# A hybrid decoder layer on one core: another order for the first 125 microseconds

## The chip, the cores and the metric

One core of a Trainium2 chip runs the whole layer. The core has a matmul engine (TensorE, PE in the profile, with PEld for its weight loads), three engines for elementwise work (VectorE or DVE, ScalarE or ACT, GpSimd or POOL) and SyncE (SP), which here issues nearly all the transfers. Each engine works through its own instruction queue in order and waits on semaphores for the others. The metric is the device time of one execution in microseconds.

## The reference

```python
mod = silu(c) @ w_ada + b_ada                 # c: 2048, w_ada: 2048 x 6144
shift, scale, gate = split(mod, 3)
h = rms_norm(x, norm_gain) * (1 + scale) + shift        # x: 1024 tokens x 2048
proj = h @ w_in                                # w_in: 2048 x 8192
# columns: q, k, v, z of 8 stick-breaking heads, then q, k, v, z of 8 retention heads
qa, ka = rms_norm(q_sb) * sb_q_gain, rms_norm(k_sb) * sb_k_gain
oa = stick_breaking_attention(qa, ka, v_sb) * silu(z_sb)
ob = head_group_norm(retention(rotary(q_r), rotary(k_r), v_r)) * silu(z_r)
out = x + gate * (concat(oa, ob) @ w_out)      # w_out: 2048 x 2048
```

Everything is float32. Nothing of h can be had before shift and scale, which need 2048 rows of w_ada, and before the norm of x; and no projection starts before some of h is there.

## The kernel before, in words

**The projections.** A projection is done by a Strassen-Winograd scheme: one `Group` makes 256 output columns for all 1024 tokens over half of the contraction (1024 of 2048), as seven products P1 to P7 of combinations of blocks. The left operands are the seven combinations A11, S2, S3, A12, S1, A22, S4 of h, the right ones combinations of the weights (`RIGHT`, `LEFT`). Each combination of h is cut into four pieces `j` (`NP` = 4) and each piece into a high and a low part in fp32r (`split`: the high part by ScalarE, the low part, the rest, by VectorE), and so are the weights (`first` makes the high part, `second` the low part, `make` the sums). A product of one piece is three matmuls (`mm3`: high by high, high by low, low by high), a product of a group twelve. Products share PSUM banks: P1, P6, P5 and P3 add into bank b, P7 and P4 into d, P2 has bank a; after P1, P6 and P7 ScalarE copies the bank out (`ended`, `copied`) before the next product goes into it. `plan` writes the products of all groups in one list: P1, then P4 and P3 of the group before, then P6, P7, P2, P5. Weights are split two products ahead of their use, with three buffers.

**The opening** is what stands before that list. A piece j of h needs four 512-token by 128-channel tiles xT (two channel blocks, two token halves g), and scale and shift for those 256 channels. The steps:

- 32 tiles of x are loaded (`xt`), each 128 tokens by 512 channels, into places that are later used for the parts of h.
- `x_norms(g)` takes the mean squares of 4 times 128 tokens, half by ScalarE (`Square` with a sum), half by VectorE (`bn_stats`), makes the inverse root by Newton steps on VectorE (`rsqrt_newton`), and puts it on a diagonal (`dg`), in two pairs of 128 tokens.
- `turn_x(kc, g)` transposes four 128 by 128 blocks of x on TensorE against those diagonals, which also multiplies by the norm; ScalarE or, each fourth time, VectorE copies the result to xT.
- For each j, `ada_loads` loads 16 tiles of w_ada ("rows" below: 128 of the 2048 rows of w_ada, 256 columns of shift and 256 of scale). Each is weighed by silu(c): six by VectorE (`ADA_DVE`, `weigh`, line 443) into an accumulator, two by ScalarE with a sum on GpSimd (`ADA_ACT`), eight by TensorE, which sums over its partitions at once (`ada_rows_pe`, line 526). `ada_finish` adds TensorE's one row of sums to the accumulator and sums over partitions by matmuls against ones (`over_partitions`), so that the sums stand in columns; `ada_mod` makes scale and shift from them.
- `first_half(j)` applies them (`to_h`, line 435, on ScalarE), makes the combinations (`combine`, on GpSimd for j up to 2, on VectorE for the last) and the high and low parts (`place`).

The tiles of w_ada share places: eight for block 0, ten for each later block, for sixteen rows. SyncE issues the loads in its queue's order and waits at one whose place isn't free.

**What sets the order.** In the opening only TensorE's instructions run in the order in which they are written; those of the other engines are put in order by a scheduler with its own estimate of the times. From the first `until` on all engines run as written. The list's own work hangs on a count: `tick` is called after each piece of a product, and starts tasks that wait for their turn, among them the second half of w_ada's rows and of h (`second_half`). `prepare(0)` runs those events of the list that lie before its first product: loads of the first two groups' weights, sums and splits.

Of the kernel before, what the change touches and what calls it, by code (L numbers as in the profile page):

```python
# [11 lines left out]
F32 = mybir.dt.float32  # L12
# [28 lines left out]
ADA_DVE = (0, 3, 6, 8, 11, 14)  # L41
ADA_ACT = (5, 13)
# [17 lines left out]
def layer_kernel(ctx, tc, x, c, w_ada, b_ada, norm_gain, w_in, sb_q_gain, sb_k_gain, ret_norm_gain, w_out,  # L60
# [4 lines left out]
    ctx.enter_context(tc.manual_schedule(engines={mybir.EngineType.PE}))  # L65
# [34 lines left out]
    k1 = k1p.__enter__()  # L100
    stp = tc.tile_pool(name="st", bufs=1)
# [5 lines left out]
    silu_c = cons.tile([P, 16], F32, name="silu_c")  # L107
    nc.scalar.activation(silu_c, c_sb, AF.Sigmoid)
    nc.vector.tensor_tensor(silu_c, silu_c, c_sb, op=ALU.mult)

# [9 lines left out]
    nc.scalar.dma_start(rows[66:74, 0:P], ret_norm_gain.rearrange("o (k p) -> (o k) p", p=P))  # L120
    rows_ps = ps.tile([P, P], F32, tag="C", name="rows_ps")
# [82 lines left out]
    def combine(a11, a12, a21, a22, new, sub):  # L204

        s1, s2, s4 = (new(n) for n in ("S1", "S2", "S4"))
        sub.tensor_tensor(s1, a21, a22, op=ALU.add)
        sub.tensor_tensor(s2, s1, a11, op=ALU.subtract)
        sub.tensor_tensor(a21, a11, a21, op=ALU.subtract)
        sub.tensor_tensor(s4, a12, s2, op=ALU.subtract)  # L210
        return {"A11": a11, "S3": a21, "S2": s2, "A12": a12, "S1": s1, "S4": s4, "A22": a22}

# [21 lines left out]
    class Group:  # L234


        def __init__(self, w, k0, col0, name, **more):
            self.w, self.k0, self.col0, self.name = w, k0, col0, name
            self.seed, self.gate, self.put, self.done, self.pool, self.turns = None, (None, None), None, None, None, False
            self.before = None  # L240
            self.__dict__.update(more)
            self.t, self.parts, self.at, self.old, self.tell, self.early = {}, {}, {}, {}, None, None
# [24 lines left out]

    sums = []
# [36 lines left out]
    def plan(groups, lasts):  # L305
# [16 lines left out]
        for k, (g, p) in enumerate(flat):  # L322
            if p == "P1":
                on(k - 7, 0, lambda g=g: g.load(0))
                on(k - 6, 1, lambda g=g: g.load(1))
                sum_of(g, "T3", k - 3, 1)
                alone = g.at["P6"] == k + 1
                sum_of(g, "T2", k - 2 if alone else k - 1, 3 if alone else 1)
# [95 lines left out]
    def ada_mod(j, mod):  # L424
# [6 lines left out]
    ENGINES = [mybir.EngineType.PE, mybir.EngineType.Activation, mybir.EngineType.DVE, mybir.EngineType.Pool,  # L431
               mybir.EngineType.SP]

# [22 lines left out]

    turns = 0

    def turn_x(kc, g):

        nonlocal turns
        tag, bufs = (("pj0", 1), ("A1", 1), ("pj1", 1), ("pj2", 1), ("B", 1), ("pj3", 1))[turns % 6]
        turns += 1
        tp = ps.tile([P, HALF], F32, tag=tag, bufs=bufs, name=f"xtp_{kc}_{g}")
# [14 lines left out]
    def x_norms(g):  # L479
        for t2 in (4 * g, 4 * g + 2):  # L480
            ss = st.tile([P, 4], F32, tag="ss", bufs=2, name=f"ss_{t2}")
            st6 = st.tile([P, 4, 6], F32, tag="st6", bufs=2, name=f"st6_{t2}")
            mv = st.tile([P, 2], F32, tag="mv", bufs=2, name=f"mv_{t2}")
            for qt in range(4):
                junk = st.tile([P, HALF], F32, tag="ht", bufs=7, name=f"junk_{t2}_{qt}")
                nc.scalar.activation(junk, xt[t2, qt], AF.Square, accum_out=ss[:, qt:qt + 1])
            for qt in range(4):
                nc.vector.bn_stats(st6[:, qt, :], xt[t2 + 1, qt])
            nc.vector.bn_aggr(mv, st6)
            m = st.tile([P, 2], F32, tag="m", bufs=2, name=f"m_{t2}")  # L490
            y = st.tile([P, 2], F32, tag="y", bufs=2, name=f"y_{t2}")
            u = st.tile([P, 2], F32, tag="u", bufs=2, name=f"u_{t2}")
            nc.vector.tensor_reduce(m[:, 0:1], ss, axis=mybir.AxisListType.X, op=ALU.add)
            nc.vector.tensor_scalar(m[:, 0:1], m[:, 0:1], 1.0 / D, EPS, op0=ALU.mult, op1=ALU.add)
            nc.vector.scalar_tensor_tensor(m[:, 1:2], mv[:, 0:1], mv[:, 0:1], mv[:, 1:2], op0=ALU.mult, op1=ALU.add)
            nc.vector.tensor_scalar(m[:, 1:2], m[:, 1:2], EPS, None, op0=ALU.add)
            rsqrt_newton(y, m, u)
            for i in range(2):
                dg[t2 + i] = st.tile([P, P], F32, tag="dg", bufs=8, name=f"dg_{t2 + i}")
                nc.vector.tensor_scalar(dg[t2 + i], ident, y[:, i:i + 1], None, op0=ALU.mult)  # L500

    accs, acc2s, for_pe, row_sums = {}, {}, {}, {}

    def ada_loads(j):

        accs[j] = acc = st.tile([P, HALF], F32, tag="acc", bufs=2, name=f"acc_a{j}")
        tags = free[0][:8] if j == 0 else free[j]
        for r in range(16):
            src = hp.tile([P, HALF], F32, tag=tags[r % len(tags)], name=f"ada_a{j}_{r}")
            nc.sync.dma_start(src.rearrange("p (a n) -> p a n", a=2), ada_rows[:, r, 0:2, 256 * j:256 * j + 256])  # L510
            if r in ADA_DVE:
# [855 lines left out]
```

## Time and profile before

| | |
|---|---|
| median of 3 runs | 2012.84 us (2012.56 to 2014.52) |
| the profiled execution | 2010.2 us, of which the profile's span is 2008.4 us |
| granted TensorE clock, mean over the span | 0.983 |
| TensorE busy | 1932.5 us, 96% |
| VectorE busy | 1460.3 us, 73% |
| ScalarE busy | 866.7 us, 43% |
| GpSimd busy | 189.6 us, 9% |
| HBM read and written | 278.51 and 108.10 MB |

The page gives for each engine its busy time, cuts the span into 40 slices of 50 us with busy tenths and the granted clock in tenths, and lists the costliest groups of instructions. A row of the view in order of time has the start, the duration, the engine, the line, the operation, the tile written and those read, the shape, the count of instructions that were merged, and in brackets the idle time of the engine before it and what ended it. Instructions of TensorE overlap, so the distance of their starts is what one costs, not the duration. The table by stretches gives busy times in windows.

### The profile page before, as it was taken

To read this page: it belongs to the slowest core of one execution; us is meant where nothing else is said; L and a number is where in the kernel's file an instruction comes from. 1 tells how busy PE (TensorE), PEld (TensorE's weight loads), DVE (VectorE), ACT (ScalarE), POOL (GpSimd) and SP (SyncE) were. 2 spreads that over 40 slices of the span, in tenths; PEclk is the share of its full clock that TensorE was granted. 3 is DMA by queue.
4 is the path that set the end of the run, shared out by engine and by line. 5 is a ranking of instruction groups with operands and counts; after the bars stand their busy time and mean duration, and the time that the engine had idled before them with its cause. 6 is when DMAs were issued, how large, how long until landed. Compare 5 with 4: busy or idle time off the path is not lost. (4 is left out here: it accounts for less than half of the span.)

```text
span 2008.4 us, 26769 instructions
## 1 busy us (share of the span) xinstructions
PE 1932.5 (96%) x9057; PEld 1557.8 (78%) x9057; DVE 1460.3 (73%) x2598; ACT 866.7 (43%) x1574; POOL 189.6 (9%) x131
## 2 busy tenths in 40 slices
PE   5879999999999999999999999899999998999998
PEld 4368888876778787788888888588888887888887
DVE  6778898685668586766656766688787887568765
ACT  4443333553354544454444444434343445345221
POOL 0311111220000001001000100113021211010000
PEclk9879999999999999999999999899999999999999
DMA  9738988434545455443433534758677887357665
GB/s 298 248 119 274 291 283 300 132 110 125 184 152 156 129 169 185 144 133 108 155 114 124 169 104 131 269 189 287 205 265 242 274 273 259 127 168 262 204 206 167
DMA packets 287325, 388.41 MB, mean 193 GB/s; under 512 B 32106, under 2 KB 164276, under 8 KB 287188
## 3 DMA queue, kind: packets, MB, share of 16 engines
q1 hardware_dynamic: 286784, 386.65, 59.5%
q8 instruction: 72, 1.18, 0.3%
q14 instruction: 65, 0.53, 0.1%
q10 hardware_dynamic: 404, 0.05, 0.0%
HBM read 278.51 MB, written 108.10 MB: 192 GB/s over the span
## 5 line engine op out<-in xcount | busy, mean ns | idle before, releaser
L259 ACT ACTIVATE wh_e_P<-wr_e 128x512 fp32r<-128x512 f32 x560 | 353.0, 631 | 464.5 <-PE b_o L151 55.3
L264 DVE TENSOR_TENSOR wl_e_P<-wr_e,wh_e_P 128x512 fp32r<-128x512 f32 x560 | 402.1, 718 | 90.6 <-ACT wh_e_P L259 89.2
L254 DVE TENSOR_TENSOR wr_e<-wr_e,wr_e 128x512 f32<-128x512 f32 x240 | 167.8, 726 | 1.3
L917 DVE TENSOR_TENSOR_SCAN om<-om 128x128 f32<-128x128 f32 (+2 forms) x96 | 95.8, 998 | 55.7 <-ACT om L908 54.1
L443 DVE SCALAR_TENSOR_TENSOR acc_b<-ada_b,silu_c,acc_b 128x512 f32<-128x512 f32 x120 | 90.0, 750 | 17.9 <-DMA ada_b<-in_w_ada_dram 17.1
L730 POOL TENSOR_TENSOR ld<-ld,ld 128x512 f32<-128x512 f32 x7 | 10.3, 1468 | 980.7 <-DMA ld<-mix_A 980.7
L292 DVE TENSOR_TENSOR pt<-b_f,pt 128x512 f32<-128x512 f32 x64 | 44.1, 689 | 57.4 <-PE b_f L152 57.2
L150 PE MATMUL b_e<-S_h,wh_e_P 128*128 128x512 f32 x192 | 76.5, 398 | 5.7 <-ACT pt L286 5.7
L150 PE MATMUL b_h<-S_h,wh_e_P 128*128 128x512 f32 x192 | 78.1, 407 | 1.5 <-ACT S_h L146 1.5
L152 PE MATMUL b_e<-S_h,wl_e_P 128*128 128x512 f32 x192 | 75.9, 396 | 1.2 <-DVE wl_e_P L264 1.2
L964 PE MATMUL oT<-a,v 128*128 128x256 f32 x320 | 76.8, 379 | 0.0
L150 PE MATMUL b_f<-S_h,wh_e_P 128*128 128x512 f32 x192 | 76.6, 399 | 0.0
L151 PE MATMUL b_h<-S_l,wh_e_P 128*128 128x512 f32 x192 | 76.2, 397 | 0.2 <-DVE S_l L147 0.2
L152 PE MATMUL b_h<-S_h,wl_e_P 128*128 128x512 f32 x192 | 75.9, 395 | 0.3 <-DVE wl_e_P L264 0.3
L151 PE MATMUL b_e<-S_l,wh_e_P 128*128 128x512 f32 x192 | 75.8, 395 | 0.0
L150 PE MATMUL b_g<-S_h,wh_e_P 128*128 128x512 f32 x192 | 75.6, 394 | 0.0
L908 ACT ACTIVATE om<-zp,rq 128x128 f32<-128x128 f32 (+2 forms) x96 | 56.0, 583 | 44.9 <-PE zp L903 39.7
L151 PE MATMUL b_f<-S_l,wh_e_P 128*128 128x512 f32 x192 | 75.0, 390 | 0.0
L152 PE MATMUL b_g<-S_h,wl_e_P 128*128 128x512 f32 x192 | 75.0, 390 | 0.0
L152 PE MATMUL b_f<-S_h,wl_e_P 128*128 128x512 f32 x192 | 75.0, 390 | 0.0
L151 PE MATMUL b_g<-S_l,wh_e_P 128*128 128x512 f32 x192 | 74.9, 390 | 0.0
L286 ACT ACTIVATE pt<-b_e 128x512 f32<-128x512 f32 x48 | 28.8, 599 | 97.2 <-PE b_e L152 94.1
(389 smaller groups left out, 5250.0 us busy)
## 6 DMA issues: line engine op xcount, KB each, us to landing
wr_e<-in_w_in_dram SPq DMA_DIRECT2D x128, 512.0 KB
ada_b<-in_w_ada_dram SPq DMA_DIRECT2D x128, 256.0 KB
part<-pt SPq DMA_DIRECT2D x128, 256.0 KB
pt<-part SPq DMA_DIRECT2D x128, 256.0 KB
fin<-pt SPq DMA_DIRECT2D x128, 256.0 KB
ada_a<-in_w_ada_dram SPq DMA_DIRECT2D x64, 256.0 KB
wr_e<-in_w_out_dram SPq DMA_DIRECT2D x32, 512.0 KB
ld<-fin SPq DMA_DIRECT2D x54, 256.0 KB
```

The source lines that it names most:

```text
L150: nc.tensor.matmul(o, a_hi, b_hi, start=first, stop=False, skip_group_check=True)
L151: nc.tensor.matmul(o, a_hi, b_lo, start=False, stop=False, skip_group_check=True)
L152: nc.tensor.matmul(o, a_lo, b_hi, start=False, stop=last, skip_group_check=True)
L254: eng.tensor_tensor(t[o], t[a], t[b], op=op)
L259: nc.scalar.activation(hi, self.t[RIGHT[p]], AF.Copy)
L264: nc.vector.tensor_tensor(lo, self.t[RIGHT[p]], self.parts[p].bitcast(F32), op=ALU.subtract)
L286: nc.scalar.activation(t, src, AF.Copy, scale=1.0 if gt is None else gt)
L292: nc.vector.tensor_tensor(t, src, t, op=ALU.add)
L443: nc.vector.scalar_tensor_tensor(acc, src, cj, acc, op0=ALU.mult, op1=ALU.add)
L908: nc.scalar.activation(om[:, :n], zp[:, :n], AF.Sigmoid, scale=rq[:, h, 1, i:i + 1])
L917: nc.vector.tensor_tensor_scan(rev, rev, rev, init, op0=ALU.mult, op1=ALU.bypass)
L964: nc.tensor.matmul(ob, v[:, j, :], a[:, cl], start=diag and ib == 0 and b == 0 and j2 == 0, stop=ch == 0 and ib == 2, skip_group_check=True)
```

## The change

It writes the opening anew. All engines run in written order from the start (`manual_schedule` with all five). The steps go into a list `todo` with a time each (`do(us, fn, ...)`), and are written in the order of these times, which count a tile of x or w_ada each 0.8 us (`landed`).

- w_ada: VectorE weighs four rows of a block (1, 4, 7, 10; in block 0 three: 9, 11, 13), TensorE the other twelve (thirteen), ScalarE and GpSimd none. `ada_close` adds VectorE's accumulator to the sums by one more matmul against ones, and ScalarE copies the row of sums; `ada_turn` turns it into columns with four small matmuls instead of `over_partitions`. There is one accumulator place instead of two.
- Norms: one Newton chain for four times 128 tokens instead of two, the squares are written to a PSUM bank, four diagonals instead of eight.
- `first_left` takes the place of `first_half` and `combine`: the combinations are all VectorE's, written between the parts; in the last block VectorE also makes two of the four tiles of h.
- The first group's products come in the order P1, P2, P7, P6, P5, and P1, P2 and P7 run by pieces: pieces 0 and 1, then 2, then 3, between the rows of w_ada. The weights of the first group are loaded between those of blocks 1 and 2, those of the second after block 3; `prepare(1)` splits the weights for the first three products.
- The small constants are loaded ahead of the sigmoid of c on ScalarE's queue. The result tiles (`sums`) have their place from the start.

```diff
-ADA_DVE = (0, 3, 6, 8, 11, 14)
-ADA_ACT = (5, 13)
+ADA_DVE = (1, 4, 7, 10)
+ADA_DVE_0 = (9, 11, 13)
...
-    ctx.enter_context(tc.manual_schedule(engines={mybir.EngineType.PE}))
+    ctx.enter_context(tc.manual_schedule(engines=set(ENGINES)))
...
             flat.append((g, "P1"))
-            if i:
-                flat.extend((groups[i - 1], p) for p in ("P4", "P3"))
+            if not i:
+                flat.extend((g, p) for p in ("P2", "P7", "P6", "P5"))
+                continue
+            flat.extend((groups[i - 1], p) for p in ("P4", "P3"))
             flat.extend((g, p) for p in ("P6", "P7", "P2", "P5"))
...
+    def do(us, fn, *a):
+        todo.append((us, len(todo), lambda: fn(*a)))
+
+    def landed(n):
+
+        return 3.5 + 0.8 * (n + 1)
...
+    def ada_row(j, r):
+
+        src, on_dve = row_tiles.pop((j, r)), ADA_DVE if j else ADA_DVE_0
+        if r in on_dve:
+            if r == on_dve[0]:
+                accs[j] = st.tile([P, HALF], F32, tag="acc", bufs=1, name=f"acc_a{j}")
+            weigh(accs[j], src, r, r == on_dve[0])
+            return
+        if r == 0:
+            row_sums[j] = ps.tile([P, HALF], F32, tag=("C", "A0")[j % 2], name=f"ada_sums{j}")
+        nc.tensor.matmul(row_sums[j][0:1, :], silu_c[:, r:r + 1], src, start=r == 0, stop=False, skip_group_check=True)
+
+    def ada_close(j):
+
+        nc.tensor.matmul(row_sums[j][0:1, :], ones, accs[j], start=False, stop=True, skip_group_check=True)
+        nc.scalar.activation(accs[j][0:1, :], row_sums.pop(j)[0:1, :], AF.Copy)
+
+    def ada_turn(j):
+
+        mod, acc = ps.tile([P, 4], F32, tag="B", name=f"mod_m{j}"), accs.pop(j)
+        for i in range(4):
+            nc.tensor.matmul(mod[:, i:i + 1], acc[0:1, i * P:(i + 1) * P], ones[0:1, :], start=True, stop=True)
+        ada_mod(j, mod)
...
+    def first_left(j, us):
+
+        a11, a21, a12, a22 = (xT[2 * j + e, g] for e in range(2) for g in range(2))
+        last = j == NP - 1
...
+        do(us, to_h, a11, 2 * j)
+        do(us, to_h_dve if last else to_h, a12, 2 * j + 1)
+        do(us + 0.1, place, "A11", j, a11)
+        do(us + 0.2, to_h, a21, 2 * j)
+        do(us + 0.2, to_h_dve if last else to_h, a22, 2 * j + 1)
+        do(us + 0.3, place, "A12", j, a12)
+        do(us + 1.0, lambda: tt(s1, a21, a22, op=ALU.add))
+        do(us + 1.0, lambda: tt(a21, a11, a21, op=ALU.subtract))
+        do(us + 1.1, lambda: tt(s2, s1, a11, op=ALU.subtract))
+        do(us + 1.2, place, "S3", j, a21)
+        do(us + 1.3, place, "S2", j, s2)
+        do(us + 2.0, place, "S1", j, s1)
+        do(us + 3.0, lambda: tt(s4, a12, s2, op=ALU.subtract))
+        do(us + 4.0, place, "A22", j, a22)
+        do(us + 5.0, place, "S4", j, s4)
...
+    x_norms(0, landed(15) + 1)
+    x_norms(1, landed(31) + 1)
     for kc in range(KC):
-        turn_x(kc, 0)
...
+        do(21.5 + 0.56 * kc, turn_x, kc, 0)
+        do(35.0 + 0.5 * kc if kc < KC // 2 else 42.0 + kc - KC // 2, turn_x, kc, 1)
+
+    at_row = [32, 48, 68, 84]
+    for j in range(NP):
+        for r in range(16):
+            us = landed(at_row[j] + r)
+            do(us - 4, ada_load, j, r)
+            do(us + 0.3, ada_row, j, r)
+        us = landed(at_row[j] + 15) + 0.5
+        do(us, ada_close, j)
+        do(us + 1.5, ada_turn, j)
+        do(us + 2.5, lambda j=j, us=us: first_left(j, us + 2.6))
+    for i in range(2):
+        do(landed(63) - 3.9, groups_a[0].load, i)
+        do(landed(99) - 3.9, groups_a[1].load, i)
+    do(landed(63) + 12, prepare, 1)
...
+    do(landed(63) + 14, first_products, (0, 1))
+    do(landed(83) + 11, first_products, (2,))
...
+    first_products((3,))
+    run_to[0] = 3
```

`first_products(js)` runs `mm3` for the pieces js of P1, then of P2, then of P7; with the last piece it also ends each product as `run` does.

More of the change, by code (lines that the diff above doesn't have):

```diff
@@ L100, in layer_kernel @@
     k1 = k1p.__enter__()
+    pp = ctx.enter_context(tc.tile_pool(name="pp", bufs=1))
+    sums = [pp.tile([P, HALF], F32, tag=f"pt{i}", bufs=1, name=f"pt{i}") for i in range(7)]
     stp = tc.tile_pool(name="st", bufs=1)
@@ L202, in layer_kernel @@
     left = {}
[L204 to L211, printed above, removed]
     def place(n, j, src, eng=nc.vector):
@@ new lines, in layer_kernel, with first_products @@
+    do(landed(63) + 12, prepare, 1)
+    def first_products(js):
+        g = groups_a[0]
+        for k, (p, into, i) in enumerate((("P1", "b", 0), ("P2", "a", 3), ("P7", "d", 2))):
+            if js[0] == 0:
+                setattr(g, into, bank(i, f"{into}_{g.name}"))
+            hi, lo = g.parts[p]
+            for j in js:
+                mm3(getattr(g, into), hi[:, j, :], lo[:, j, :], *left[LEFT[p], j], j == 0, j == NP - 1)
+            if js[-1] == NP - 1:
+                ended(g, p)
+                for j in range(NP):
+                    for fn in events.pop((k, j), ()):
+                        fn()
+                tick()
```

150 lines of the change are left out of this document (56 added, 94 removed).

## The prediction

> **What bounds the kernel now.** First the page: engines and clock.
>
> ```profile
> span 2008.4 us, 26769 instructions
> PE 1932.5 (96%) x9057; PEld 1557.8 (78%) x9057; DVE 1460.3 (73%) x2598; ACT 866.7 (43%) x1574; POOL 189.6 (9%) x131
> PEclk9879999999999999999999999899999999999999
> ```
>
> TensorE is the bound over the whole span, but slices 2 and 3 (50 to 150 us) have a clock of 0.8 and 0.7. So I looked at the opening in stretches of 10 us, and in stretches of 2 us where the clock changes (columns: length, busy time of PE, PEld, DVE, ACT, POOL, granted clock, DMA share, GB/s).
>
> ```profile
> 80.00:90.00 10.00, 7.38 (x24) 2.04 (x24) 8.51 (x12) 6.03 (x10) 5.37 (x4) 0.97 0.76 247
> 90.00:100.00 10.00, 5.37 (x18) 3.57 (x18) 9.84 (x13) 3.99 (x7) 2.30 (x2) 0.50 0.46 152
> 100.00:110.00 10.00, 7.59 (x25) 6.22 (x25) 6.40 (x11) 6.94 (x11) 6.32 (x4) 0.50 0.00 1
> 130.00:140.00 10.00, 10.00 (x46) 8.29 (x45) 7.75 (x13) 3.50 (x6) 0.00 (x0) 1.00 0.62 190
> ...
> 88.00:90.00 2.00, 0.53 (x2) 0.00 (x0) 2.00 (x3) 0.96 (x3) 2.00 (x2) 0.87 1.07 374
> 90.00:92.00 2.00, 0.00 (x0) 0.00 (x0) 2.00 (x3) 1.57 (x3) 1.19 (x2) 0.50 0.31 104
> 126.00:128.00 2.00, 2.00 (x8) 1.60 (x7) 0.00 (x0) 0.46 (x1) 0.00 (x0) 0.74 0.16 55
> ```
>
> Between 80 and 110 us VectorE is the fullest engine (9.84 of 10 us), TensorE has holes, and its clock is halved from about 89.5 to 127 us. From 130 us on TensorE is full and does the same work in both kernels. I therefore reduce the question to one mark: the first matmul of the second group's P1, when the first group's P1, P6, P7, P2 and P5 are done whatever their order. TensorE in order of time shows the mark and what comes before it.
>
> ```profile
> 103.91 0.77 PE L150 MATMUL b_e<-A_h,wh_e_P 128*128 128x512 f32 x1
> 107.46 0.63 PE L152 MATMUL b_e<-A_h,wl_e_P 128*128 128x512 f32 x1
> 122.29 0.79 PE L150 MATMUL b_e<-S_h,wh_e_P 128*128 128x512 f32 x1 [5.67 <-ACT pt L286]
> 122.88 0.63 PE L151 MATMUL b_e<-S_l,wh_e_P 128*128 128x512 f32 x1
> 123.31 0.63 PE L152 MATMUL b_e<-S_h,wl_e_P 128*128 128x512 f32 x1
> 127.34 0.40 PE L150 MATMUL d_e<-S_h,wh_e_P 128*128 128x512 f32 x1
> 130.07 0.39 PE L150 MATMUL a_e<-A_h,wh_e_P 128*128 128x512 f32 x1
> 135.51 0.39 PE L150 MATMUL b_e<-A_h,wh_e_P 128*128 128x512 f32 x1
> ```
>
> The mark is at 135.5 us. P6 starts at 122.3; its matmuls start 0.43 us apart (122.88 to 123.31) at half clock, and a product of 12 matmuls takes 2.73 us at full clock (127.34 to 130.07), 0.2275 each.
>
> **Prices of the parts.** TensorE's opening work, in order of time, and SyncE's last load of a w_ada row:
>
> ```profile
> 21.53 22.73 PE L467 MATMUL xtp<-dg,x 128*128 128x128 f32 x188 [5.99 <-DMA x<-in_x_dram]
> 53.99 7.41 PE L467 MATMUL xtp<-dg,x 128*128 128x128 f32 x64
> 61.24 1.84 PE L421 MATMUL mod_m<-ones,acc_a 128*128 128x1 f32 x16
> 63.02 12.18 PE L526 MATMUL ada_sums<-ada_a,silu_c 128*1 128x512 f32 x28
> 78.22 1.02 PE L526 MATMUL ada_sums<-ada_a,silu_c 128*1 128x512 f32 x2 [1.80 <-DMA ada_a<-in_w_ada_dram]
> 87.51 1.02 PE L526 MATMUL ada_sums<-ada_a,silu_c 128*1 128x512 f32 x2 [1.15 <-DMA ada_a<-in_w_ada_dram]
> 93.87 1.86 PE L526 MATMUL ada_sums<-ada_a,silu_c 128*1 128x512 f32 x2 [5.34 <-DMA ada_a<-in_w_ada_dram]
> ...
> 90.99 0.37 SPq L510 DMA_DIRECT2D ada_a<-in_w_ada_dram  x1
> ```
>
> One row of w_ada on TensorE is two matmul instructions: 12.18 / 14 = 0.87 us. One turn of x (turn_x) is eight: (61.24 - 53.99) / 8 = 0.91. ada_turn has four matmuls, eight instructions, where 16 took 1.84: 0.92. A reloaded row can be used 93.87 - 90.99 = 2.9 us after its issue. VectorE and ScalarE, in order of time:
>
> ```profile
> 21.19 0.48 DVE L500 TENSOR_SCALAR dg<-ident,y 128x128 f32<-128x128 f32 x2
> 63.40 0.48 DVE L441 TENSOR_SCALAR acc_a<-ada_a,silu_c 128x512 f32<-128x512 f32 x1
> 63.91 2.33 DVE L443 SCALAR_TENSOR_TENSOR acc_a<-ada_a,silu_c,acc_a 128x512 f32<-128x512 f32 x3
> 118.86 0.68 DVE L147 TENSOR_TENSOR S_l<-S,S_h 128x512 fp32r<-128x512 f32 x1
> 119.47 0.68 DVE L147 TENSOR_TENSOR A_l<-xT,A_h 128x512 fp32r<-128x512 f32 x1
> ...
> 63.52 2.93 ACT L435 ACTIVATE xT<-xT,s_c,a_c 128x512 f32<-128x512 f32 x4 [2.37 <-DVE a_c L428]
> 66.35 1.13 ACT L146 ACTIVATE A_h<-xT 128x512 fp32r<-128x512 f32 x2
> 120.19 0.63 ACT L146 ACTIVATE S_h<-S 128x512 fp32r<-128x512 f32 x1 [2.41 <-DVE A_l L147]
> 121.64 0.60 ACT L286 ACTIVATE pt<-b_e 128x512 f32<-128x512 f32 x1 [0.82 <-DVE S_l L147]
> ```
>
> VectorE: 0.6 an operation (119.47 - 118.86), 0.78 a weighed row, 0.5 a block's first. ScalarE: 0.73 to make h, 0.56 a high part.
>
> **The change part by part, on TensorE's queue.** Rows on TensorE go from 8 a block to 13 in block 0 and 12 after: 49 in all instead of 32. That alone is 17 x 0.87 = 14.8 us more on the engine that in the new order also has to do everything else in sequence. What it saves is on engines with room: two rows of ScalarE and their sum on GpSimd, two or three rows of VectorE.
>
> (1) Start. The four factors of tokens 0 to 511 now come from one Newton chain after the sixteenth tile of x, as the later pair's do now (21.19, 0.24 each); two more of them make it 21.8 for a start that is now at 21.53.
>
> (2) To the end of ada_close(1): 32 turns x 0.91 = 29.1; 13 + 12 rows x 0.87 = 21.8; two closes at a row's price, 1.7; ada_turn(0), 0.9. The first matmuls run at half speed, by the tile's own windows:
>
> ```profile
> 22.00:24.00 2.00, 2.00 (x11) 2.00 (x11) 0.00 (x0) 0.60 (x1) 1.00 1.05 385
> 25.00:27.00 2.00, 2.00 (x20) 2.00 (x19) 0.23 (x1) 0.39 (x2) 1.00 1.05 393
> ```
>
> (11 against 20 in 2 us, though the clock column says 1.00): some 1.4 us for the first three. Sum 54.9, so 76.7. The close needs VectorE's row 10, which is written behind the 11 operations that place block 0, an evacuation and two rows: an estimate of 0.8 us late, 77.5.
>
> (3) ada_turn(1) waits for ScalarE's copy (0.6 and hand-over, 0.7), then 0.92: 79.1.
>
> (4) Then the queues bite. TensorE goes on with seven rows of block 2 and stands at row 11 at 79.1 + 7 x 0.87 = 85.2. Row 11 uses the buffer of row 1, which is VectorE's, and VectorE's row 1 is written behind block 1's A11 and A12 and its three sums and S3, S2. That is: bias and scale 0.45, ScalarE's four to_h and two high parts 4.0, VectorE's A12 low part and three sums 2.4, two low parts with a short wait 1.35, the row 0.5: done at 87.8. SyncE waits there with that load; rows 12 to 15, block 3's rows and group 1's weights queue behind it. Plus 2.9: row 11 is there at about 90.8, and TensorE has idled 5.6 us.
>
> (5) After that the clock is halved, as after 88.53 us now. From 122.29 it took 4.4 us to recover, so I charge 2.2. Rows 11 and 12, 18 product matmuls for blocks 0 and 1 (4.1), rows 13 to 15, the close, block 3's row 0 and ada_turn(2) are 11.1: 90.8 + 11.1 + 2.2 = 104.1. VectorE's five operations for the first three weights (prepare) end at about the same time as row 11 comes; if their cover went, they would cost up to 3.4.
>
> (6) Eight rows, block 2's nine matmuls (2.05), three rows, the close: 12.5. Two waits of the kind in (4) come again, for row 14's reload and VectorE's row 10, an estimate of 2.6 from the same 11 operations and three rows. 119.2; copy and ada_turn(3): 120.8.
>
> (7) Last block. Bias 0.45, to_h 0.73, high part 0.56, ten VectorE operations of 0.6 and one of 0.5, then S4's high part, which waits for A22's low part as in the row at 120.19, then three more (S4, T1 and P6's weights): 11.4 with hand-overs. P6's second matmul at 132.2. Ten or eleven at half clock, 4.1; then ScalarE must copy P6 out of the bank that P5 goes into, which no product stands between any more: 0.7; P5, 2.73. The mark comes at 139.8.
>
> So the mark moves from 135.5 to 139.8: +4.3 us. The sum stands against the profiled execution: 2010.2 us for a span of 2008.4, so 2014.5. The median of the three runs, 2012.84, is 2.6 above it; on that scale 2017.1, and I forecast 2017.
>
> In that sum P2 and P7 are a gain (24 x 0.2275 = 5.5: they lie ahead of P6 in time that waits anyway), the last chain is 7 us shorter than now (11.4 against 104.1 to 122.3), and bias and scale of block 3 come 17 us later (121.2 against 104.1):
>
> ```profile
> 104.08 0.16 DVE L427 TENSOR_TENSOR a_c<-mod_m,scale_b 128x2 f32<-128x2 f32 x1 [3.60 <-PE mod_m L421]
> ```
>
> Costed at nothing: the constants' DMAs moved ahead of the sigmoid on ScalarE's queue and the squares into PSUM (covered by the x loads to 21 us; uncovered, at most a few 0.6 us activations); the empty GpSimd queue; group 1's weights, loaded last (TensorE needs them only after 139; uncovered 2.9); the second half's loads, starting three products later (they have hundreds of us). VectorE's first row of blocks 1 and 3 must wait for the ada_turn before it (one accumulator): VectorE is idle there.
>
> Bounds of the unknown prices: the gap of (4) between 0 (row ready in time) and 5.6 plus the 5.3 which the wait at 93.87 shows; the clock's loss between 0 (after the 1.80 us gap before 78.22 it stayed at 1.00) and half speed to the end. I take the gap by the order written and the recovery by the row at 122.29, which is the same kind of dense work.
>
> A rule that speaks against the change. The row first: the clock had fallen by about 89.5 (0.87 over 88 to 90), one us after the matmul of 87.51 ended. The Trainium skill (TensorE: Matmul & The Clock Gate, Part 1) says that the clock is halved after one idle window of about 3.4 us, free-running, and restored after a busy one, so that gaps over about 3 us are to be avoided. By that rule the 5.6 us gap could miss a whole window; by the trace less than a whole idle window is enough. That difference is the rival R2.
>
> **Rivals.**
> R1, not slower: VectorE gets to the freed buffers in time, so TensorE never waits for a reload. Then the gap (5.6), its clock loss (2.2) and the other waits (0.8 + 2.6) go: 11.2 less, mark at 128.6, 2012.84 - 6.9 = 2005.9. For it: VectorE has no GpSimd beside it and 0.6 is its best rate. Against: the row would have to be done by 85.2 - 2.9 = 82.3, 5.5 us earlier than its place in the queue allows. It decides from about 4 us of that.
> R2: the clock never falls. 2.2 go in (5), of which the waits in (6) take back some 1.5, and 1.9 of P6: mark about 137.2, 2014.5.
> R3, slower: the clock doesn't recover between the rows, as it didn't in the dense matmuls from 103.91 to 108.1, at 0.50 throughout. Then 17 rows and a close cost 15.7 more and 27 matmuls 5.4, less the 4.8 that are counted or hidden: +16, 2033.
> R4, the change does what its times say: DMA sets the pace, the last row at the written 83.8, mark at 83.8 + 0.9 + 1.6 + 19 = 105.3, 1982.6. Against it: TensorE's own list (32 turns, 49 rows, three closes and turns of sums, 27 products' matmuls) is 83 us from 21.8 on, before that close.
>
> **How the numbers follow.** Forecast 0.49 (own range 2012 to 2022), R1 0.22, R2 0.12, R3 0.12, R4 0.05. Within 0.2% (4 us, about what a measurement here can tell) lie a third of the forecast, two thirds of R2 and a fifth of R1: 0.28. Faster: most of R1, R4 and a tail of the forecast, 0.26. Slower 0.46. The range 2004 to 2027 takes in R1 and the lower part of R3 and leaves out R4 and the rest of R3.
>
> **What would show it.** In the new profile: matmuls of w_ada's rows 0.87 us a row from 36 us on without DMA being full; a wait of TensorE of 5 to 6 us for a w_ada load between 85 and 91, with SyncE's issue right behind a VectorE row; a clock of 0.50 behind it; first product matmuls at about 93; bias and scale of block 3 at 121; P6 at 131 to 132; the mark at 139.8. A last close before 112 would make the forecast wrong to the fast side, a clock of 0.50 at 105 to the slow side.

## The result and the profile after

The changed kernel takes 2021.14 us (median of 6 runs, 2018.77 to 2023.89) against 2012.7 us before (6 runs, 2007.57 to 2016.82). The ratio on record is 1.0055, 95% interval 1.0042 to 1.0069; the two medians alone give 1.0042. By that interval it is slower by 8 to 14 us. The prediction's mark, the first matmul of the second group's P1, moved from 135.51 to 147.67 us: +12.2, where +4.3 was forecast. The span grew by 11.1 us, so the loss lies ahead of the mark, and the question is why the opening lost three times what its steps added up to.

The page of the kernel after:

```profile
span 2019.5 us, 26746 instructions
PE 1948.0 (96%) x9067; PEld 1550.9 (77%) x9067; DVE 1448.6 (72%) x2579; ACT 861.3 (43%) x1568; POOL 164.7 (8%) x115
PEclk9979999999999999999999999899999999999999
```

TensorE is busy for 15.5 us more; 17 more rows of w_ada at 0.87 are 14.8. Its clock is now low only in the third slice (100 to 150 us), but TensorE isn't full there either. The same opening in stretches of 10 us (columns as in the prediction):

```profile
80.00:90.00 10.00, 8.97 (x27) 2.06 (x25) 3.24 (x9) 4.55 (x7) 0.00 (x0) 1.00 0.89 290
90.00:100.00 10.00, 5.20 (x12) 1.94 (x12) 9.84 (x17) 4.57 (x8) 0.00 (x0) 0.83 0.60 179
100.00:110.00 10.00, 10.00 (x36) 4.17 (x35) 0.88 (x5) 1.41 (x3) 0.00 (x0) 1.00 0.75 244
120.00:130.00 10.00, 6.08 (x19) 2.81 (x18) 5.33 (x12) 3.88 (x6) 0.00 (x0) 0.82 0.26 88
130.00:140.00 10.00, 5.64 (x11) 3.10 (x11) 9.21 (x14) 5.43 (x10) 1.51 (x1) 0.50 0.08 28
140.00:150.00 10.00, 9.31 (x29) 6.88 (x28) 4.06 (x7) 1.75 (x3) 0.00 (x0) 0.66 0.48 152
```

The third busy column is VectorE. It goes 3.24, 9.84, 0.88 in the first three stretches: it stands mostly idle, then fills a whole stretch while TensorE is half empty, then is idle again. Two engines take turns instead of working side by side. The clock is at 0.50 from about 126 to 147 us (worked out from these rows in the last section). TensorE in order of time, with what ended its waits:

```profile
23.95 16.18 PE L471 MATMUL xtp<-dg,x 128*128 128x128 f32 x128 [9.50 <-DVE dg L510]
46.39 1.02 PE L535 MATMUL ada_sums<-ada_a,silu_c 128*1 128x512 f32 x2
47.34 1.16 PE L471 MATMUL xtp<-dg,x 128*128 128x128 f32 x8
48.43 1.02 PE L535 MATMUL ada_sums<-ada_a,silu_c 128*1 128x512 f32 x2
74.79 6.17 PE L535 MATMUL ada_sums<-ada_a,silu_c 128*1 128x512 f32 x14
80.79 1.02 PE L539 MATMUL ada_sums<-acc_a,ones 128*1 128x512 f32 x2
83.47 4.54 PE L535 MATMUL ada_sums<-ada_a,silu_c 128*1 128x512 f32 x10
95.04 3.02 PE L535 MATMUL ada_sums<-ada_a,silu_c 128*1 128x512 f32 x4 [4.80 <-DMA ada_a<-in_w_ada_dram]
108.16 7.03 PE L535 MATMUL ada_sums<-ada_a,silu_c 128*1 128x512 f32 x16
122.24 1.02 PE L539 MATMUL ada_sums<-acc_a,ones 128*1 128x512 f32 x2 [1.21 <-DVE acc_a L437]
123.94 1.05 PE L546 MATMUL mod_m<-ones,acc_a 1*128 1x1 f32 x8 [0.68 <-ACT acc_a L540]
135.76 0.79 PE L156 MATMUL b_e<-S_h,wh_e_P 128*128 128x512 f32 x1 [2.86 <-ACT wh_e_P L256]
137.77 0.79 PE L158 MATMUL b_e<-S_h,wl_e_P 128*128 128x512 f32 x1 [0.79 <-DVE wl_e_P L261]
143.09 0.79 PE L156 MATMUL b_e<-S_h,wh_e_P 128*128 128x512 f32 x1 [0.69 <-ACT pt L281]
147.67 0.39 PE L156 MATMUL b_e<-A_h,wh_e_P 128*128 128x512 f32 x1
```

Three places matter here: the start at 23.95 behind an idle time that VectorE ended; the wait of 4.80 us for a load of w_ada, ended at 95.04; and the row that I call the last turn below, the turn of block 3's sums at 123.94, behind which P6 comes 11.8 us later. VectorE and ScalarE around the wait, in order of time:

```profile
79.48 0.75 DVE L437 SCALAR_TENSOR_TENSOR acc_a<-ada_a,silu_c,acc_a 128x512 f32<-128x512 f32 x1
83.57 0.16 DVE L424 TENSOR_TENSOR a_c<-mod_m,scale_b 128x2 f32<-128x2 f32 x1 [3.35 <-PE mod_m L546]
86.10 0.69 DVE L153 TENSOR_TENSOR A_l<-xT,A_h 128x512 fp32r<-128x512 f32 x1 [2.10 <-ACT A_h L152]
91.96 0.48 DVE L435 TENSOR_SCALAR acc_a<-ada_a,silu_c 128x512 f32<-128x512 f32 x1
```

VectorE waits 3.35 us for the sums and 2.10 for ScalarE; its first row of block 2 (91.96) is written behind both, though TensorE used the row after it from about 84.3 (83.47 + 0.87); and the load into that row's place comes to TensorE 2.6 us after it ended. Step (4) said this.

### The profile page after: what moved, and what is told of

It is laid out like the page before. It is cut to its first block, busy times and chain, and to the rows that moved or that the text cites. A ratio compares the mean times of both kernels' runs of the same rounds, so it can differ in the third digit from the quotient of the medians.

```text
span 2019.5 us, 26746 instructions
## 1 busy us (share of the span) xinstructions
PE 1948.0 (96%) x9067; PEld 1550.9 (77%) x9067; DVE 1448.6 (72%) x2579; ACT 861.3 (43%) x1568; POOL 164.7 (8%) x115
## 5 line engine op out<-in xcount | busy, mean ns | idle before, releaser
L967 DVE TENSOR_TENSOR_SCAN om<-om 128x128 f32<-128x128 f32 (+2 forms) x96 | 95.6, 995 | 55.8 <-ACT om L958 54.2
L780 POOL TENSOR_TENSOR ld<-ld,ld 128x512 f32<-128x512 f32 x7 | 10.5, 1497 | 978.7 <-DMA ld<-mix_A 978.7
```

The source lines that it names most:

```text
L967: nc.vector.tensor_tensor_scan(rev, rev, rev, init, op0=ALU.mult, op1=ALU.bypass)
```

## The experiments

All ratios are to the kernel before, in the same set of runs; the kernel before had medians of 2012.7, 2008.4, 2010.4 and 2009.6 us in the four sets. "Mark" and "last turn" are read from TensorE in order of time.

A mark comes from one trace, and the traces scatter. Seven of these kernels (after, a1_free, a2_last, a12_both, a8_warm, a5_early, a9_vec) have the same code up to the first row of w_ada on TensorE, and reach it at 40.06, 40.99, 40.54, 41.27, 40.79, 41.43 and 40.81 us. The first turns of x run at half speed for a while that differs from run to run: TensorE does 9 and 14 instructions from 24 to 26 and 26 to 28 us in after, and 20 from 28 to 30; in a5_early it does 8, 12 and 11. So up to 1.4 us of a difference between two marks needn't come from the edit; where it matters, I count from that first row.

| kernel | edit | ratio (95%) | last turn, us | mark, us |
|---|---|---|---|---|
| before | | 1 | | 135.51 |
| after | | 1.0055 (1.0042 to 1.0069) | 123.94 | 147.67 |
| a1_free | VectorE's rows where nothing reuses their place | 1.0072 (1.0058 to 1.0087) | 127.98 | 149.85 |
| a2_last | pieces 0 to 2 behind the last turn | 1.0055 (1.0041 to 1.0069) | 121.44 | 145.22 |
| a12_both | both | 1.0041 (1.0029 to 1.0053) | 121.60 | 142.35 |
| a3_start | small loads on SyncE behind x | 1.0050 (1.0038 to 1.0062) | 120.38 | 144.11 |
| a8_warm | 22 unread matmuls in the last chain | 1.0050 (1.0037 to 1.0063) | 124.78 | 144.73 |
| b1_rows | kernel before, only the rows moved | 1.0006 (0.9996 to 1.0016) | | 134.99 |
| a5_early | a2, VectorE's rows and first weights early | 0.9986 (0.9976 to 0.9995) | 110.31 | 132.34 |
| a9_vec | a5, pieces between the rows as in after | 1.0016 (1.0005 to 1.0026) | 115.93 | 137.92 |
| a6_all | a5, a3 and more rows on VectorE | 0.9975 (0.9965 to 0.9984) | 107.95 | 131.85 |
| a7_best | a6 with fewer of them, 10 unread matmuls | 0.9962 (0.9951 to 0.9972) | 104.26 | 124.21 |

**Is it the reload that TensorE waits for?** Step (4) blamed the buffer that VectorE's row frees late. In a1_free VectorE takes rows whose places no later row of the same block needs.

```diff
-ADA_DVE = (1, 4, 7, 10)
+ADA_DVE = (6, 7, 8, 9)
```

> VectorE weighs rows 6 to 9 of blocks 1 to 3, whose places no later row of the block takes. Theory V (VectorE's queue in written order is what holds TensorE in block 2, whatever it waits for first): the wait for a w_ada load before row 11 (4.8 us in the changed kernel's trace) goes, but TensorE then stands at the first product, whose weights' low part VectorE makes behind block 1's placing and the same four rows; that product starts at 98 to 99 us as now, the mark stays within 2 us of 147.7, the time within 0.15% of the changed kernel's 2021. Theory L (the late load itself is the cost): the first product starts at 92 to 93, the mark moves to 140 to 143, the time to 2014 to 2016.

The wait for the load fell from 4.80 to 0.21 us, but the mark came 2.2 us later (1.25 counted from the first row). TensorE of a1_free in order of time:

```profile
90.89 2.73 PE L535 MATMUL ada_sums<-ada_a,silu_c 128*1 128x512 f32 x6 [0.21 <-DMA ada_a<-in_w_ada_dram]
96.99 0.50 PE L156 MATMUL b_e<-A_h,wh_e_P 128*128 128x512 f32 x1 [3.36 <-ACT wh_e_P L256]
101.16 0.80 PE L158 MATMUL b_e<-A_h,wl_e_P 128*128 128x512 f32 x1 [3.43 <-DVE wl_e_P L261]
```

TensorE now stands at the next thing that VectorE owes it, the first weights' split (`prepare(1)`), which is written behind the same placing and rows: 6.8 us in two waits instead of 4.8 in one. Theory L falls. V stands for what it says of the wait; of its numbers, the first product started at 96.99 and not at 98 to 99, and the mark lies 0.2 us outside its range. The DMA named as releaser was only the messenger of VectorE's queue.

**Is it the products between the rows?** In a2_last the pieces 0 to 2 of P1, P2 and P7 are written after the last turn; TensorE then doesn't need the split weights early.

```diff
-    do(landed(63) + 14, first_products, (0, 1))
-    do(landed(83) + 11, first_products, (2,))
...
+    first_products((0, 1, 2))
     first_products((3,))
```

> The pieces 0 to 2 of P1, P2 and P7 are written behind the last block's sums instead of between the rows of w_ada. Theory T (TensorE's list sets when block 3's scale and shift come): the 27 matmuls, 7.5 us with their edges, leave the list, so the last sums end at 117 to 118 us instead of 125; they then lie in the 11 us in which TensorE waits for block 3's operands, and keep its clock up; the mark comes at 136 to 138, the time at 2009 to 2012. Rival D (VectorE or the loads set the pace of the last blocks, and the pieces between the rows are hidden work): the last sums stay within 2 us of 125 and the mark comes at 147 to 152, the time at 2020 to 2025.

That 6.1 us of matmuls (27 x 0.2275) leave the list brought the last turn only 2.5 us forward, and both waits for reloads are there: 4.80 us ended at 95.74, and a new one of 3.28 at 116.10. So T is missed. D's own ranges are missed too (the last sums end at 122.5, the mark is at 145.22), but it comes nearest: VectorE, or the loads that wait for it, set the pace here.

**Both at once.** a12_both has both edits.

> Both edits. Under V and T: neither the reload nor the weights of the first product hold TensorE in block 2, so the 4.8 us wait and the lower clock behind it go as well; the last sums end at 111 to 114, the mark comes at 130 to 133, the time at 2004 to 2008, below the kernel before. Under D, no better than the products at the end alone. Under L with T, the sum of the two gains, 129 to 132: the two theories agree here and differ at the first edit alone.

Missed: from 90 us to the last turn no wait for a load or a weight over 0.73 us is left, and yet the last turn is at 121.60. TensorE of a12_both:

```profile
100.23 1.02 PE L539 MATMUL ada_sums<-acc_a,ones 128*1 128x512 f32 x2 [3.23 <-DVE acc_a L437]
119.06 1.87 PE L539 MATMUL ada_sums<-acc_a,ones 128*1 128x512 f32 x2 [4.80 <-DVE acc_a L437]
```

Now the closes wait for VectorE's accumulator. Between two closes (18.8 us) VectorE's queue holds the bias, a wait of 2.10 and one of 1.24 for ScalarE's h, eleven placing operations, and among and behind them the four rows of the next block: a loop through three engines. Whatever TensorE is spared, it gets to the next close before VectorE does. The idea of two separate waits, each worth its own gain, fell here; what stands is VectorE's order.

**Take VectorE's rows out of that loop.** a5_early is a2_last with VectorE's rows of blocks 2 and 3 made rows 0 to 3, which land early, and written ahead of the placing, where VectorE waits for ScalarE; with two accumulators; and with the first weights loaded 16 rows of w_ada earlier in SyncE's order and split 12 us earlier in the list.

```diff
-ADA_DVE = (1, 4, 7, 10)
-ADA_DVE_0 = (9, 11, 13)
+ADA_DVE = ((9, 11, 13), (1, 4, 7, 10), (0, 1, 2, 3), (0, 1, 2, 3))
...
-                accs[j] = st.tile([P, HALF], F32, tag="acc", bufs=1, name=f"acc_a{j}")
+                accs[j] = st.tile([P, HALF], F32, tag="acc", bufs=2, name=f"acc_a{j}")
...
-            do(us + 0.3, ada_row, j, r)
+            early = j > 1 and r in ADA_DVE[j]
+            do((57.85, 73.85)[j - 2] if early else us + 0.3, ada_row, j, r)
...
-        do(landed(63) - 3.9, groups_a[0].load, i)
+        do(landed(47) - 3.9, groups_a[0].load, i)
...
-    do(landed(63) + 12, prepare, 1)
+    do(landed(63), prepare, 1)
```

> Products at the end as before, and VectorE's queue freed: its rows of blocks 2 and 3 are rows 0 to 3, written where it waits for ScalarE to make the h of the block before, with two accumulators; the first three weights are loaded and split before block 1's placing. The number of rows on each engine is that of the changed kernel. Theory V2 (after the products at the end alone, the way from one block's sums to the next goes through VectorE's placing and the rows behind it, 15 us a block): TensorE has no wait over 1 us between 85 and 108, block 3's sums end at 108 to 113 instead of 122.4, the mark comes at 129 to 135, the ratio to the kernel before is 0.996 to 1.000. Rival T (TensorE's list alone sets block 3's sums): they end at 118 to 122, the mark at 139 to 145, ratio 1.003 to 1.006.

Against a2_last the last turn is 11.1 us earlier and the mark 12.9. Same stretches, a5_early:

```profile
80.00:90.00 10.00, 9.32 (x29) 2.49 (x28) 8.68 (x16) 6.43 (x11) 0.00 (x0) 1.00 0.93 302
90.00:100.00 10.00, 9.05 (x28) 2.32 (x27) 7.32 (x16) 4.67 (x8) 0.00 (x0) 1.00 0.98 324
```

VectorE is busy for 8.68 and 7.32 where it was 3.24 and 9.84, TensorE is full, DMA is nearly full, and the clock stays up. From 84 us to the last turn TensorE waits only 0.28 us for a load and 0.68 for each copy of the sums. V2 stands, T falls: with VectorE's order put right, TensorE's list sets the time.

**What are the pieces between the rows worth?** a9_vec is a5_early with the products where the changed kernel has them.

> The early VectorE rows and the early split of the first weights, but the products of blocks 0 to 2 between the w_ada rows again, as in the changed kernel. Theory Q (the pairs are worth nothing there: with VectorE early TensorE waits for nothing, so 27 matmuls x 0.23 = 6.2 us lie in its list ahead of the last sums, and the chain behind those sums takes the same 13.8 us to P6's second matmul): turn of block 3's sums at 116 to 117 instead of 110.3, the mark at 138 to 139 instead of 132.3, ratio to before 1.0010 to 1.0025. Rival W (the products fill holes that the loop from sums to sums leaves, and keep the clock up): turn of block 3's sums by 112, the mark within 2 us of 132.3, ratio 0.998 to 0.999.

The last turn comes 5.6 us later than in a5_early, the mark 5.6 us later, the ratio goes from 0.9986 to 1.0016: theory Q, nearly to the number. Counted from the first row the mark moves by 6.2 us, the price of the 27 matmuls (6.1). Once VectorE keeps up, running the products by pairs of blocks puts 27 matmuls into a list that is already full, ahead of the sums on which everything waits, while the chain behind the last turn would have had room for them. That chain takes 13.8 us here, in a5_early and in after alike, up to the first matmul with the low part of P6's weights, which I call P6's second part. The difference between after and a9_vec, 9.8 us of mark (10.5 from the first row), is VectorE's order: its rows, the split of the weights with their earlier load, and the second accumulator, which no run parts.

**The start.** a3_start issues the five small loads from SyncE behind x and turns them later.

```diff
-    nc.scalar.dma_start(rows[0:16, 0:P], norm_gain.rearrange("o (k p) -> (o k) p", p=P))
...
+    do(25.0, load_rows)
+    do(29.0, turn_rows)
```

> The five small loads of gains and biases go to SyncE's queue behind x, and are turned and used later; nothing else moves. The first turn of x started at 23.95 us, after squares that began at 13.2 behind those loads on ScalarE's queue, and statistics that began at 15.1. Theory S (that order cost the start): squares begin at about 4.5, statistics at about 8.5, the first turn at 21.3 to 22; as TensorE's list follows without slack, the mark moves by 2 to 2.5 us to 145 to 146, the time to about 2019. Rival (x's sixteenth tile sets the start, or the waits later swallow it): first turn at 23 or later, or mark at 147 to 148.

Theory S stands, and more came off than it said: the turns of x start at 19.78 instead of 23.95, the last turn and the mark come 3.6 us earlier. ScalarE and VectorE of after show why:

```profile
6.41 0.34 ACTq L119 DMA_DIRECT2D rows<-in_norm_gain_dram  x1
11.46 0.28 ACTq L123 DMA_DIRECT2D rows<-in_ret_norm_gain_dram  x1
11.77 1.28 ACT L125 ACT_TABLE_LOAD   x1 [11.77 <-DMA rows<-in_b_ada_dram]
13.19 0.58 ACT L492 ACTIVATE junk<-x 128x512 f32<-128x512 f32 x1
13.32 0.17 DVE L126 TENSOR_TENSOR silu_c<-silu_c,c_sb 128x16 f32<-128x16 f32 x1 [11.60 <-ACT silu_c L125]
14.49 0.24 DVE L129 COPY cols<-rows_ps 128x74 f32<-128x74 f32 x1 [1.00 <-PE rows_ps L128]
15.11 2.46 DVE L495 BATCH_NORM_STATS2 st<-x 128x6 f32<-128x512 f32 x4
```

The five issues end at 11.74, and the sigmoid and the first square stand behind them. VectorE is held twice: its product for silu(c) waits for the sigmoid, and its copy of the constants, turned by TensorE, for the last of the loads. Its statistics of x stand behind both, and from 15.11 it works without a wait to the diagonals at 23.61; ScalarE's eighth square is over at 19.2, and VectorE takes its sums at 20.99 without waiting. So the late start ends on VectorE's written order too. In a3_start the first square is at 4.28 and the statistics start at 7.97. No run parts the two holds. The kernel before had the same five loads behind three squares, and its fourth waited for them:

```profile
11.35 0.63 ACT L486 ACTIVATE junk<-x 128x512 f32<-128x512 f32 x1 [3.55 <-DMA rows<-in_b_ada_dram]
```

The ratio of a3_start, 1.0050, can't be told from 1.0055; the trace can.

**The clock in the last chain.** a8_warm adds matmuls whose result nobody reads: 8 ahead of P1's last piece, 3 ahead of P7's, 11 ahead of P6.

> The changed kernel with 22 matmuls more whose result nobody reads, in the places where TensorE waits in the last block (8 before piece 3 of P1, 3 before that of P7, 11 before P6). Theory C (the halved clock of P6 and P5, 0.43 us a matmul instead of 0.23, is 4 to 5 us of the mark, because TensorE is idle in the last chain): P6 and P5 run at 0.23 a matmul, the mark moves from 147.7 to 143 to 145, the time by -0.15 to -0.25% against the changed kernel. Rival: the clock falls all the same or the added matmuls hold up the chain: mark 147 to 150.

A stretch of a8_warm, and two rows of its TensorE:

```profile
130.00:140.00 10.00, 7.12 (x27) 4.68 (x28) 9.18 (x14) 5.44 (x10) 1.51 (x1) 1.00 0.00 1
138.62 0.50 PE L158 MATMUL b_e<-S_h,wl_e_P 128*128 128x512 f32 x1 [1.28 <-DVE wl_e_P L261]
144.73 0.39 PE L156 MATMUL b_e<-A_h,wh_e_P 128*128 128x512 f32 x1
```

Theory C stands: the clock stays at 1.00 from the last turn to the mark, P6's second part is as late as in after behind the last turn (13.84 us, 138.62 - 124.78), and from there to the mark it takes 6.1 us instead of 9.9. The mark is 2.9 us earlier, though this run's last turn was 0.8 later; 0.7 of that it already had at the first row. The ratio, 1.0050, is too near 1.0055 to show it.

**Do the rows themselves cost?** b1_rows is the kernel before with only the rows shared out as in the change: VectorE four, TensorE twelve, ScalarE and GpSimd none.

```diff
-ADA_DVE = (0, 3, 6, 8, 11, 14)
-ADA_ACT = (5, 13)
+ADA_DVE = (1, 4, 7, 10)
```

> The kernel before with one part of the change alone: VectorE weighs rows 1, 4, 7, 10 of each block, TensorE the other twelve, ScalarE and GpSimd none; order and everything else as before. TensorE gets 16 rows more, 13.9 us, less half of the matmuls against ones, 3.7. Theory H (in the order of before TensorE has holes between 76 and 122 us that take them, while VectorE gets lighter): mark 133 to 138, ratio 0.998 to 1.002. Rival (a row on TensorE costs its 0.87 us wherever it is): mark 144 to 147, ratio 1.004 to 1.006.

The mark is at 134.99, the ratio 1.0006, and 1 lies within the interval. H stands: in the order of before, sixteen rows more on TensorE cost nothing that these runs can tell. TensorE waits for no load in b1_rows between 60 and 125 us, where the kernel before waited 1.80, 1.15 and 5.34 (the prediction's rows at 78.22, 87.51 and 93.87): the extra rows fall into that time. Its clock is also 1.00 from 80 to 100 us, where the kernel before had 0.97 and 0.50. So the loss isn't the rows alone; it is what the order written out by hand makes of them.

**All remedies, and the version that beats both.** a6_all is a5_early with a3_start's loads and more rows on VectorE.

```diff
-ADA_DVE = ((9, 11, 13), (1, 4, 7, 10), (0, 1, 2, 3), (0, 1, 2, 3))
+ADA_DVE = ((8, 9, 10, 11, 13, 14), (4, 5, 6, 7, 8, 9), (0, 1, 2, 3), (0, 1, 2, 3))
```

> As the run beside it, with the start mended (small loads on SyncE) and VectorE weighing six rows in blocks 0 and 1, five rows less on TensorE. With VectorE out of the way TensorE's list should count now: 5 x 0.87 = 4.4 and 2.2 to 2.5 of the start come off, so block 3's sums end 6 to 7 us before those of the run beside it, the mark at 122 to 128, the ratio to the kernel before 0.993 to 0.997. If VectorE still sets the pace, only the start or less comes off: mark within 3 us of the run beside it.

Missed: the mark is at 131.85, only 0.5 ahead of a5_early's, although the turns of x start 4.2 us earlier. Close 1 waits 1.93 us for VectorE's accumulator, the clock falls there (0.83 over 70 to 80 and over 80 to 90 us), and it falls again in P6 and P5 (0.55 over 120 to 130). a7_best gives TensorE back two rows each of blocks 0 and 1 and puts ten unread matmuls ahead of P6.

```diff
-ADA_DVE = ((8, 9, 10, 11, 13, 14), (4, 5, 6, 7, 8, 9), (0, 1, 2, 3), (0, 1, 2, 3))
+ADA_DVE = ((9, 10, 11, 13), (4, 5, 6, 7), (0, 1, 2, 3), (0, 1, 2, 3))
...
     first_products((3,))
+    keep_warm(10)
```

> The kernel with all the remedies together: early VectorE rows and weights, products of blocks 0 to 2 last, small loads on SyncE behind x, four VectorE rows a block (9, 10, 11, 13 in block 0; 4 to 7 in block 1; 0 to 3 in blocks 2 and 3), and ten unread matmuls ahead of P6. Theory Z (two VectorE rows fewer in blocks 0 and 1 take away the wait of 1.9 us for VectorE at close 1 and the clock's fall behind it, about 3.4 us, for four rows x 0.87 = 3.5 us more on TensorE; and the unread matmuls save the half clock of P6 and P5, about 20 x 0.2 = 4 us less the 0.7 that they may add): turn of block 3's sums at 107 to 109, clock 1.0 to the mark, the mark at 127.5 to 129.5, ratio 0.9950 to 0.9965. Rival Y (the wait for VectorE or the half clock comes back at another place): the mark at 131 or later, ratio 0.997 or more.

TensorE of a7_best in order of time:

```profile
77.70 1.05 PE L535 MATMUL mod_m<-ones,acc_a 1*128 1x1 f32 x8 [1.75 <-ACT acc_a L529]
104.26 1.05 PE L535 MATMUL mod_m<-ones,acc_a 1*128 1x1 f32 x8 [0.68 <-ACT acc_a L529]
113.57 2.43 PE L630 MATMUL warm<-A_h 128*128 128x512 f32 x10
118.10 0.50 PE L146 MATMUL b_e<-S_h,wl_e_P 128*128 128x512 f32 x1 [1.28 <-DVE wl_e_P L249]
124.21 0.39 PE L144 MATMUL b_e<-A_h,wh_e_P 128*128 128x512 f32 x1
```

Median 2000.97 us against 2009.59 before; the ratio, 0.9962, is inside what was written down, the last turn and the mark are some 3 us earlier than the ranges. The close of block 1 no longer waits for VectorE, but its turn for ScalarE's copy of the sums (1.75 us, ahead of 77.70); four rows more on TensorE cost less than the freed wait and clock brought. The mark is 23.5 us ahead of after's, and the parts measured one at a time come to nearly as much: VectorE's order 9.8, the pieces 5.6, the start 3.6, the clock 2.9, 21.9 in all. The agreement is no proof: each part carries the scatter of its traces, a7_best also shares out the rows of blocks 0 and 1 otherwise, and a6_all shows that such gains need not add.

## Why the prediction was right or wrong

The direction and the mechanism held; the size didn't. The forecast of 2017 lay 4 us under the median, and 0.2% was forecast where 0.55% was measured. By steps, with what each missed by on its own:

| step | forecast | measured | its own error |
|---|---|---|---|
| (1) turns start | 21.8 | 23.95 | +2.2 |
| (2) end of ada_close(1) | 77.5 | 81.8 | +2.2 |
| (3) end of ada_turn(1) | 79.1 | 83.5 | +0.1 |
| (4) row 11 | 90.8 | 95.04 | -0.2 |
| (5) end of ada_turn(2) | 104.1 | 108.2 | -0.1 |
| (6) end of ada_turn(3) | 120.8 | 125.0 | +0.1 |
| (7) P6's second part | 132.2 | 137.77 | +1.4 |
| (7) mark | 139.8 | 147.67 | +2.3 |

**Right: (3) to (6).** The wait for the reload was forecast at 5.6 and measured at 4.80, and from ada_turn(1) to row 11 it took 11.5 us where 11.7 was reckoned (the terms as written add up to 11.6). It was found by following one load back to the buffer it needs, to the row that frees it and to what is written ahead of that row. But the step took the buffer for the cause. a1_free shows that without it the same queue holds the weights, and a12_both that without either it holds the closes. In (6) the sum came out right although its waits did not: 1.5 us of waits for loads and accumulator instead of 2.6.

**Wrong: "costed at nothing", the constants' DMAs.** The text named the x loads as cover up to 21 us. They cover DMA time, not the queues: ScalarE was held until 11.74, and VectorE's statistics, which the factors need, stood until 15.11 behind the sigmoid and the turned constants. It cost 2.2 us against step (1), and a3_start gets 4.2 back, more than was lost: 21.8 was reckoned from the start before, where the same loads held ScalarE for 3.55 us. The two more diagonals in (1) should not have been counted: TensorE starts 0.34 us after the first diagonal's operation does, in both kernels (21.19 to 21.53, 23.61 to 23.95).

**Wrong: (2), 0.87 and 0.91 for every row and turn.** Those prices hold within a run of the same kind (14 instructions, seven rows, at 74.79 take 6.00 to the next). In the changed list rows and turns alternate, and a single row then takes 0.95 (46.39 to 47.34), a single turn 1.09 (47.34 to 48.43). About a dozen changes of kind make 3 us; the 0.8 that I charged for a late close 1 wasn't there.

**Mis-sized: (7), the last chain.** 12.8 us from the last turn instead of 11.4: VectorE waits 0.96 for ScalarE's high part, and the low part of P6's weight takes 1.77 (135.94 to 137.71) instead of 0.6. GpSimd's first operation since the start of the layer runs beside it, from 135.65 to 137.16. The same overlap, with 1.77 again, stands in a5_early and a7_best; no run moves it, so that the one slows the other is not shown. Then the clock: I charged half speed to ten or eleven matmuls of P6, but it held through P5 as well, and P6's second part to the mark took 9.9 instead of 7.6. (Ten or eleven at 0.43 would have been 4.3 to 4.7, not 4.1.) The text's own bound, "half speed to the end", was the nearer one for this place.

**Rivals.** R1 (VectorE in time) didn't come; its price was also too simple, since a1_free met its condition and became no faster. a9_vec, which truly has VectorE in time, is still above before at 1.0016; the start, the alternation and the half clock of the last chain remain there. R2 (the clock never falls) is false in both places. R3 (it doesn't recover) is false for the rows and true for the last chain. R4 is excluded: DMA didn't set the pace of after (a share of 0.89 and 0.60 over 80 to 100 us), and even a7_best has its mark at 124.21, not 105.3. That P2 and P7 are "a gain" ahead of P6 held: in a8_warm, with 22 matmuls more on the list, P6's second part was no later behind the last turn.

**Open.** Which of its three parts makes VectorE's order worth 9.8 us is not shown. The trace of a6_all has its mark 0.5 us ahead of a5_early's and its span 3.8 us longer; that execution lay 5.5 us above the kernel's median. What differs behind the mark I haven't followed.

## What to carry to other kernels

When an engine waits for a load, follow the load to the buffer, the buffer to its reader, and then ask what else stands behind that reader in its queue: taking away only the wait that the profile names moves it to the next thing. In an order written by hand, work whose data are there early belongs into the holes in which its engine waits for others, ahead of the chain that others wait for, and work that the chain behind the last result can hide belongs behind that result. A small DMA can hold its issuing engine's queue, and with it the engines that wait for that one, even where its transfer is covered.

## What the runs showed of the hardware

**The clock comes in steps of 3.4 us, and a partly busy stretch is enough to halve it.** TensorE's granted clock in stretches of 2 us, after:

```profile
92.00:94.00 2.00, 0.00 (x0) 0.00 (x0) 2.00 (x5) 0.36 (x1) 0.00 (x0) 1.00 0.21 51
94.00:96.00 2.00, 0.96 (x2) 0.09 (x2) 1.97 (x4) 1.67 (x3) 0.00 (x0) 0.91 1.01 325
96.00:98.00 2.00, 2.00 (x4) 0.22 (x3) 1.97 (x4) 0.63 (x1) 0.00 (x0) 0.50 0.82 239
98.00:100.00 2.00, 2.00 (x8) 1.64 (x8) 2.00 (x4) 0.00 (x0) 0.00 (x0) 0.74 0.95 282
```

If the clock is either 1.00 or 0.50, 0.91 puts the fall at 95.6, after TensorE had started again, and 0.74 the recovery at 99.0: 3.4 us. The same reading of 0.82 and 0.66 in the stretches of 10 us above gives 126.4 to 146.8 us for the last chain (20.4, six times 3.4) and, for a5_early,

```profile
120.00:122.00 2.00, 0.00 (x0) 0.00 (x0) 1.30 (x3) 1.55 (x4) 0.00 (x0) 1.00 0.00 0
122.00:124.00 2.00, 1.20 (x2) 0.48 (x2) 2.00 (x2) 1.60 (x4) 1.51 (x1) 0.55 0.01 4
128.00:130.00 2.00, 1.31 (x4) 0.54 (x4) 0.03 (x1) 1.12 (x2) 0.00 (x0) 0.75 0.84 268
```

122.2 to 129.0, twice 3.4. There TensorE had stood idle for 2.37 us only, from 119.76 to 122.13. The kernel before, by the prediction's rows of 0.87 and 0.74, gives 89.5 to 127.0, 37.6 us or eleven times 3.4. The Trainium skill (TensorE: Matmul & The Clock Gate, Part 1) gives a free-running window of about 3.4 us and says that an idle window halves the clock. The lengths agree with the window; but by a5_early a hole of 2.4 us, less than a window, is enough. In a7_best a hole of 1.75 us ahead of 77.70 left the clock at 1.00.

**Alternating kinds of matmul cost** 0.08 us a row and 0.18 a turn over their prices in a run, as shown above.

**Five small loads issued from ScalarE took 5.3 us** (6.41 to 11.74) though each issue is 0.23 to 0.47 us; SyncE issued the same five in a3_start within 2.9 us, 22.04 to 24.96. They also go with slower issues on SyncE: its 32 loads of x take 23.3 to 24.5 us in the nine kernels that issue the five beside them, and 20.8 to 21.1 in the three that don't (a3_start, a6_all, a7_best). The runs don't show what stood between the issues.
